# Down projection of a hybrid decoder block: the second half takes twelve of its 22 pairs of K tiles by seven products, in natural order, seven of them with stored differences

## The chip, the cores and the metric

One core of a Trainium2 chip runs the whole kernel. The time is device microseconds of one execution, from the kernel's start to its end; lower is better. Of the kernel before there are three timed runs: a median of 1657.48 us, between 1657.41 and 1657.68.

## The reference

The reference computes one decoder block on 256 tokens with a model width of 2048, in fp32. A projection of the input feeds two attention branches, which are projected, merged under gates and added to the input, with a layer norm behind them. Then comes the gated MLP with a hidden width of 5632, in which this case lies, a second layer norm, and a small per-layer embedding (PLE):

```python
x = layer_norm(ALPHA * x + out, ...)
# gated MLP: gate path with a causal depthwise conv of width 3, then GELU
h = gelu(conv(x @ W_gate)) * (x @ W_up)          # 256 x 5632
x = layer_norm(ALPHA * x + h @ W_down, ...)      # W_down: 5632 x 2048
x = x + sigmoid(x @ W_g) * (p @ W_p)
```

(The lines are shortened to what is computed.) The down projection is `h @ W_down`.

## The kernel before

**Numbers.** TensorE multiplies in a format with a shorter mantissa than fp32. So every fp32 operand is split in two parts: ScalarE (ACT) copies it into the short format, `hi` (line 117), and VectorE (DVE) subtracts that from the original, `lo` (line 226 for a classic unit, line 200 for a seven-product unit). A product of two operands is three matmuls: hi by hi, lo by hi, hi by lo.

**Stages.** The kernel goes through the value and key projections, gates, attention, two output projections, layer norm 1, gate and up projection (44 tiles of the hidden width), down projection, layer norm 2 and PLE. Weights come from DRAM as units of 1 MiB, each a pair of blocks of 512 KB, on SP's DMA queue. That queue is in order as the program writes it: a transfer whose buffer is still in use holds all that come after it. TensorE's order is the program's, too; the orders of VectorE, ScalarE and GpSimd (POOL) come from a scheduler.

**Down projection (lines 1373 to 1391 and `s_half`, 775 to 869).** The 5632 rows of W_down are 44 K tiles, taken as 22 pairs. The 2048 output columns are two halves of 1024 (`nh` = 0, 1), one after the other; each half goes over all 22 pairs, so a unit is a pair in a half. `DN_ORDER` gives the order of the pairs in each half. A pair is computed in one of two ways:

- *classic* (line 801): 2 K tiles x 2 token tiles x 2 column tiles x 3 matmuls = 24 matmuls of 128 x 512;
- *seven products* (`strassen`, line 809), for the pairs in `DN_S`: the 2 x 2 x 2 blocks by seven products in place of eight, 7 x 3 = 21 matmuls. The left operands need sums of the hidden activations, which the gate/up stage stores in DRAM (`sd`, line 1345) and which are loaded per unit (`hS`, line 193, 512 KB). The right operands need four differences of weight blocks on VectorE (line 154). Then a unit splits a block of 512 columns (b11), one of 1024 (b2) and two of 1024 with differences (t13, t24): four ACT copies and four lo subtractions, where a classic unit has two and two.

For the pairs in `DN_T` the differences are *stored* ("parked"): during the gate/up stage `park_gen` (lines 162 to 171) loads the 1 MiB unit, makes the four differences and stores the result by POOL's queue to `td` in DRAM. In the down projection such a unit loads 256 KB of raw weight (line 181), 512 KB (line 182), the stored 1 MiB `td` (line 184) and `hS`; one without loads two blocks of 512 KB (line 188) and `hS`. The pieces of `park_gen` are pulled at steps spread over the gate/up tiles from the seventh on (lines 1349 to 1351).

After the last seven-product pair of a half, `fold` (lines 815 to 834) adds the product sums that several output blocks share: one copy and eight VectorE operations on PSUM banks (lines 818 and 819).

**Buffers and lookahead.** `unit()` (line 234) prepares units three ahead of the one in use. Raw blocks of 512 KB go to a ring of five, hi and lo parts to rings of six each. hS, td, the hidden activations hC, the residual z, the layer norm's gains and the PLE operands share a pool of 15 tiles of 8 KB per partition. In the second half the last two pairs form a tail (`end2`, line 1395) that takes them by token tile and column tile, so that the layer norm can begin early.

**Other loads in the second half (line 1457).** After position 4 the half's residual `z` (2 x 512 KB, line 1366); after 8 the gains `lnb` (2 x 1 MiB, line 1159); after 14 `ple_prep` (praw 2 x 512 KB, line 1169; pTr 256 KB, line 1174; their splits are lines 1172 and 1177). In the first half the residual of that half is loaded after position 8, and nothing else.

Positions are counted from 0 in the order of the half. In the first half of the kernel before they are the natural order, with twelve seven-product pairs, six of them parked; in the second an order written out by hand, with nine, four of them parked.

Of the kernel before, what the change touches and what calls it, by code (L numbers as in the profile page):

```python
# [23 lines left out]
NF = DFF // P  # L24
# [28 lines left out]
WO_S = ((1, 3, 5), (1, 3, 5))  # L53
WO_C = (0, 2, 4, 6, 7)

DN_ORDER = (tuple(range(NF // 2)),
            (0, 1, 2, 3, 5, 4, 8, 9, 6, 11, 7, 12, 10, 14, 13, 15, 16, 17, 18, 19, 20, 21))
DN_S = ((1, 3, 5, 6, 8, 9, 11, 12, 14, 15, 17, 18), (1, 3, 5, 8, 9, 11, 12, 14, 15))


WO_T = ((3, 5), (1, 3, 5))
DN_T = ((3, 6, 9, 12, 15, 18), (5, 9, 12, 15))
PG_ORDER = (tuple(range(8)), tuple(range(8)))
PG_S = ((), (2, 4))
AFF1 = ((0, 2, 3), (0, 2))
# [9 lines left out]
def tile_block(ctx: ExitStack, tc: tile.TileContext, wu, wfv, wpp, xT_in, x_in, pT_in, wlr,  # L75
# [25 lines left out]
    def s8(shape, dt=F32, name=None):  # L101
        return big.tile(shape, dt, tag="S8", name=name)
# [23 lines left out]
    for _ in range(8):  # L126
# [7 lines left out]
               for b, order, sset in ((52, WO_ORDER, GV_S), (68, WO_ORDER, GR_S),  # L134
                                      (120, OUT_ORDER, WO_S), (dn0, DN_ORDER, DN_S),
                                      (NU - 16, PG_ORDER, PG_S))
# [3 lines left out]
    parked = {b + nh * len(order[nh]) + order[nh].index(n): None  # L140
              for b, order, tset in ((120, OUT_ORDER, WO_T), (dn0, DN_ORDER, DN_T))
              for nh in range(2) for n in tset[nh]}
    parked = {u: i for i, u in enumerate(sorted(parked))}
    td = dr.tile([len(parked), P, 2048], F32, name="td")
    sd = dr.tile([len(DN_S[0]), P, 1024], F32, name="sd")
    hS = {}
# [26 lines left out]
    def prep_s(u):  # L173
# [15 lines left out]
        if dn0 <= u < dn0 + NF:  # L189
            nh = (u - dn0) // (NF // 2)  # L190
            pair = DN_ORDER[nh][(u - dn0) % (NF // 2)]
            hS[nh, pair] = s8([P, 4, 256], F32R, name=f"hS{nh}_{pair}")
            nc.sync.dma_start(hS[nh, pair].bitcast(F32), sd[DN_S[0].index(pair)].rearrange(
                "p (i n) -> p i n", i=4))
# [148 lines left out]
    def pull(n, gens=mixers):  # L343
        for _ in range(n):
            while gens:
                try:
                    next(gens[0])
                    break
                except StopIteration:
                    gens.pop(0)  # L350
# [397 lines left out]
    def s_sums(y):  # L748

        a11, a21, a12, a22 = [y[:, k, t * P:t * P + P] for k in range(2) for t in range(2)]  # L750
        v = t2("sums").rearrange("p (i t) -> p i t", t=P)
        for i, a, b, op in ((0, a21, a22, ALU.add), (2, a21, a11, ALU.subtract),
                            (1, v[:, 0], a11, ALU.subtract), (3, a12, v[:, 1], ALU.subtract)):
            nc.vector.tensor_tensor(v[:, i], a, b, op)
        return v
# [548 lines left out]
    for n in range(NF):  # L1304
# [21 lines left out]
        if n % 4 == 0:  # L1326
            hC[n // 4] = (s8 if n < 40 else late.tile)([P, 4, 512], F32R, name=f"hC{n // 4}")
        if pair in DN_S[0]:
            if j == 0:
# [7 lines left out]
        nc.vector.tensor_tensor(dst[:, 256:512], h, dst[:, 0:256].bitcast(F32), ALU.subtract)  # L1337
        if pair in DN_S[0] and j == 1:
            v = s_sums(yp)
            for i in range(2):  # L1340
# [3 lines left out]
                                        w[:, :, 0:P].bitcast(F32), ALU.subtract)  # L1344
                nc.gpsimd.dma_start(sd[DN_S[0].index(pair), :, 512 * i:512 * i + 512],
                                    w.rearrange("p i n -> p (i n)").bitcast(F32))
        if n >= 4:
            pull(1)
        steps = 2 * sum(map(len, DN_T))
        if n >= n0 and (n - n0) * steps // (NF - 3 - n0) != (n - n0 + 1) * steps // (NF - 3 - n0):  # L1350
# [22 lines left out]
    def down(nh, tail, mid):  # L1373
# [9 lines left out]
        def ev(t, c, ps):  # L1383
            g = 2 * nh + c
            with tc.high_priority(P_STAT if tail else 0):
# [3 lines left out]

        s_half("dn", nh, DN_ORDER[nh], DN_S[nh], cl, st, z2of, ev,  # L1390
               tail, mid, end2, 1 if tail else 3)
# [155 lines left out]
def _sst(w, orders, ssets):  # L1547


    out = []  # L1550
    for nh, (order, sset) in enumerate(zip(orders, ssets)):
        for n in order:
            b = [[w[(2 * n + j) * P:(2 * n + j + 1) * P,
                    nh * 1024 + c * 512:nh * 1024 + c * 512 + 512] for c in range(2)]
                 for j in range(2)]
            out.append(np.concatenate([b[0][1], b[0][0], b[1][1], b[1][0]] if n in sset
                                      else b[0] + b[1], 1))
    return np.stack(out)
# [11 lines left out]
def _layout(i):  # L1570
# [4 lines left out]
    for n in range(16):  # L1575
        br.append(bg[n:n + 1])
        if n % 2 == 0:
# [7 lines left out]
        + [_sst(i["w_out"][0], OUT_ORDER, WO_S), gu,  # L1585
           _sst(i["w_down"][0], DN_ORDER, DN_S),
           _sst(i["w_ple_gate"][0], PG_ORDER, PG_S)], 0)
# [43 lines left out]
```

## Time and profile before

| | |
|---|---|
| median of three timed runs | 1657.48 us (1657.41 to 1657.68) |
| the profiled execution | 1657.66 us, of which the trace's span is 1655.9 |
| mean clock granted to TensorE | 0.999 |
| TensorE busy | 1648.5 us in 8875 matmuls |
| VectorE busy | 1326.3 us |
| ScalarE busy | 904.7 us |
| DMA | 391.6 MB, mean 236 GB/s over the span |
| down projection, first half | from 1329.63 us, 111.6 us |
| down projection, second half | from 1441.20 us to PLE's first matmul at 1554.76 |

How to read it: the profile is of one execution, on whose own time any sum has to be made. A row of the timeline gives start, duration, engine, line, operation, and output <- inputs. The duration of a matmul is longer than the distance between two of them, since they are pipelined; that distance is what counts. A row of a windows view gives the window, its length, the busy time of each engine with its instructions, then the granted clock, the busy share of the 16 DMA engines and the GB/s that they moved. In the DMA view a row ends with the size of each transfer and the median time from issue to landing.

### The profile page before, as it was taken

Reading aid. Unit: us, or ns where it says so; the run is one execution under the profiler, and the core shown is the slowest. Engines: PE = TensorE matmul, PEld = TensorE weight load, DVE = VectorE, ACT = ScalarE, POOL = GpSimd, SP = SyncE. Lnnn points to the kernel's source line nnn. Section 1 sums busy time; section 2 is a strip of 40 time slices with the busy share of each in tenths; the row PEclk is TensorE's granted clock in tenths of the full one; section 3 lists DMA queues with packets and bytes.
Section 4 is the critical chain, followed back from the end, with each engine's and each line's share of the span. In section 5 each row is a group of like instructions: output and inputs, shape, how many; then the busy total and the mean of one; then the engine's idle time right before and its main releaser. Section 6 shows DMA issues by size and latency. Waiting matters only on the chain.

```text
span 1655.9 us, 24358 instructions
## 1 busy us (share of the span) xinstructions
PE 1648.5 (100%) x8875; PEld 1432.1 (86%) x8875; DVE 1326.3 (80%) x2021; ACT 904.7 (55%) x1321; POOL 73.0 (4%) x214
## 2 busy tenths in 40 slices
PE   9999999999999999999999999999999999999998
PEld 8988888888888888888898888888888888888887
DVE  7666877888989868878987877777778778987787
ACT  6655555555555654545575455555545456555553
POOL 0100000000000000000010101100111000000000
PEclk9999999999999999999999999999999999999999
DMA  8755555545656557878856787778677679898564
GB/s 323 254 163 169 171 174 171 189 157 195 205 202 207 188 170 278 302 256 296 312 175 203 271 276 265 264 241 293 239 262 259 235 267 341 288 360 314 177 222 126
DMA packets 103175, 391.60 MB, mean 236 GB/s; under 512 B 11736, under 2 KB 13024, under 8 KB 96144
## 3 DMA queue, kind: packets, MB, share of 16 engines
q1 hardware_dynamic: 97872, 362.78, 64.3%
q0 software_dynamic: 5184, 27.27, 4.4%
q8 instruction: 69, 1.13, 0.3%
q14 instruction: 50, 0.41, 0.1%
HBM read 362.74 MB, written 27.27 MB: 236 GB/s over the span
## 4 chain that ended last, share of the span: by engine, by line
PE 98%; DVE 1%; DMA 0%; ACT 0%; issue 0%; POOL 0%; SPq 0%; DVEq 0%; POOLq 0%
PE dn L797 10%; PE psu L292 10%; PE psg L292 9%; PE psm L292 7%; PE psu L294 5%; PE psg L294 5%; PE gv L797 4%; PE gr L797 4%; PE wo L797 4%; PE psm L294 4%; PE psa L292 4%; PE dn_p L797 3%; PE pg L338 3%; PE fv L457 2%; PE psa L294 2%; PE psk L292 2%
## 5 line engine op out<-in xcount | busy, mean ns | idle before, releaser
L226 DVE TENSOR_TENSOR lo<-raw,hi 128x1024 fp32r<-128x1024 f32 x486 | 590.2, 1221 | 177.5 <-ACT hi L117 175.9
L117 ACT ACTIVATE hi<-raw 128x1024 fp32r<-128x1024 f32 x486 | 511.4, 1057 | 366.0 <-issue 151.9
L292 PE MATMUL psu<-x1T,hi 128*128 128x512 f32 x688 | 240.5, 392 | 0.0
L292 PE MATMUL psg<-x1T,hi 128*128 128x512 f32 x672 | 234.9, 392 | 0.0
L294 PE MATMUL psu<-x1T,lo 128*128 128x256 f32 x688 | 192.6, 280 | 0.0
L294 PE MATMUL psg<-x1T,lo 128*128 128x256 f32 x672 | 188.1, 280 | 0.0
L292 PE MATMUL psm<-xT,hi 128*128 128x512 f32 x512 | 181.5, 397 | 0.0
L292 PEld LDWEIGHTS psu<-x1T,hi 128*128 128x128 f32 x688 | 129.2, 188 | 27.4
L292 PEld LDWEIGHTS psg<-x1T,hi 128*128 128x128 f32 x672 | 126.2, 188 | 26.8
L294 PE MATMUL psm<-xT,lo 128*128 128x256 f32 x512 | 143.4, 280 | 0.0
L294 PEld LDWEIGHTS psu<-x1T,lo 128*128 128x128 f32 x688 | 130.6, 190 | 0.0
L294 PEld LDWEIGHTS psg<-x1T,lo 128*128 128x128 f32 x672 | 127.5, 190 | 0.0
L292 PEld LDWEIGHTS psm<-xT,hi 128*128 128x128 f32 x512 | 96.3, 188 | 19.6
L797 PE MATMUL dn<-hi,hC 128*128 128x512 f32 x368 | 102.3, 389 | 0.0
L117 ACT ACTIVATE hi_t<-raw 128x1024 fp32r<-128x1024 f32 x52 | 55.2, 1062 | 80.8 <-DVE raw L154 57.9
L117 ACT ACTIVATE hi_b<-raw 128x512 fp32r<-128x512 f32 x82 | 68.7, 841 | 54.9 <-DMA raw<-in_wu_dram 12.9
L294 PEld LDWEIGHTS psm<-xT,lo 128*128 128x128 f32 x512 | 97.2, 190 | 0.2
L200 DVE TENSOR_TENSOR lo_b<-raw,hi_b 128x512 fp32r<-128x512 f32 x82 | 77.8, 953 | 15.8 <-ACT hi_b L117 15.7
L292 PE MATMUL psa<-oT,hi 128*128 128x512 f32 x256 | 89.5, 392 | 0.0
L797 PEld LDWEIGHTS dn<-hi,hC 128*128 128x128 f32 x368 | 69.0, 188 | 14.3
L200 DVE TENSOR_TENSOR lo_t<-raw,hi_t 128x1024 fp32r<-128x1024 f32 x52 | 63.5, 1222 | 10.4 <-ACT hi_t L117 8.8
L294 PE MATMUL psa<-oT,lo 128*128 128x256 f32 x256 | 71.7, 280 | 0.0
(405 smaller groups left out, 3221.7 us busy)
## 6 DMA issues: line engine op xcount, KB each, us to landing
raw<-in_wu_dram SPq DMA_DIRECT2D x553, 512.0 KB, 5.1
td<-in_wu_dram SPq DMA_DIRECT2D x15, 1024.0 KB, 8.6
td<-td POOLq DMA_DIRECT2D x15, 1024.0 KB, 6.9
td<-td SPq DMA_DIRECT2D x15, 1024.0 KB, 8.2
hS<-sd SPq DMA_DIRECT2D x21, 512.0 KB, 8.4
fvraw<-in_wfv_dram SPq DMA_DIRECT2D x13, 524.0 KB, 6.6
sd<-hs POOLq DMA_DIRECT2D x24, 256.0 KB, 6.2
lnb<-in_lng_dram SPq DMA_DIRECT2D x4, 1024.0 KB, 9.8
```

The source lines that it names most:

```text
L117: return nc.scalar.activation(o, i, AF.Copy, bias=0.0, scale=scale)
L200: nc.vector.tensor_tensor(lo, src, hi.bitcast(F32), ALU.subtract)
L226: i = nc.vector.tensor_tensor(lo, raw, hi.bitcast(F32), ALU.subtract)
L292: nc.tensor.matmul(ps, lhsT=hi[i // 8 if hoff == 0 else 0][:, w0 % 1024:w0 % 1024 + P], rhs=a[:, kt % 4, :], start=first and i == 0, stop= ...
L294: nc.tensor.matmul(ps[:, 256:512], lhsT=lo[i // 8 if hoff == 0 else 0][:, w0 % 1024:w0 % 1024 + P], rhs=a[:, kt % 4, 0:256], start=False, ...
L338: nc.tensor.matmul(bs[j][:, 0:m], lhsT=x, rhs=v[:, o:o + m], start=first and i == 0, stop=last and i == 2)
L457: nc.tensor.matmul(fbk[t][c][:, 0:n], lhsT=x, rhs=w[:, o:o + n], start=kt == 0 and i == 0, stop=kt == 15 and i == 2)
L797: nc.tensor.matmul(ps[:, e], lhsT=x, rhs=w, start=todo[id(ps)] == total[id(ps)], stop=todo[id(ps)] == 1)
```

## The change

Only three tables at the head of the file change; the code that reads them is the same.

```diff
-DN_ORDER = (tuple(range(NF // 2)),
-            (0, 1, 2, 3, 5, 4, 8, 9, 6, 11, 7, 12, 10, 14, 13, 15, 16, 17, 18, 19, 20, 21))
-DN_S = ((1, 3, 5, 6, 8, 9, 11, 12, 14, 15, 17, 18), (1, 3, 5, 8, 9, 11, 12, 14, 15))
+DN_ORDER = (tuple(range(NF // 2)), tuple(range(NF // 2)))
+DN_S = ((1, 3, 5, 6, 8, 9, 11, 12, 14, 15, 17, 18),) * 2
...
-DN_T = ((3, 6, 9, 12, 15, 18), (5, 9, 12, 15))
+DN_T = ((3, 6, 9, 12, 15, 18), (3, 6, 9, 12, 14, 15, 18))
```

The first half stays as it is. In the second half pairs 6, 17 and 18 become seven-product pairs, the order becomes the natural one, pairs 3, 6, 14 and 18 become parked and pair 5 is no longer parked (it stays a seven-product pair with its differences made on the spot). So the half has 10 classic, 5 unstored and 7 parked pairs, where it had 13, 5 and 4. There are nine matmuls fewer, and three units more that `park_gen` loads, subtracts and stores in the gate/up stage. The fold of the second half comes behind position 18, where it came behind position 15. The weights in DRAM are laid out in the order of the units, ahead of the run.

## Prediction

> **What bounds the kernel now.** I read the page's totals and its chain first, then the waits of TensorE, then the timeline of the down projection, then its windows.
>
> ```profile
> span 1655.9 us, 24358 instructions
> ...
> PE 1648.5 (100%) x8875; PEld 1432.1 (86%) x8875; DVE 1326.3 (80%) x2021; ACT 904.7 (55%) x1321; POOL 73.0 (4%) x214
> ...
> PE 98%; DVE 1%; DMA 0%; ACT 0%; issue 0%; POOL 0%; SPq 0%; DVEq 0%; POOLq 0%
> ```
> ```profile
> PE warm_ps L127 <- DVE warm L124: 1.2, 1, 1.2
> PE fv L457 <- ACT fvhi L117: 0.3, 1, 0.3
> ```
>
> TensorE is busy for the whole span, and the second fence is the complete list of its waits: both are at the kernel's start, none is in the down projection. So the time is the count of matmuls times their pitch, as long as every operand is there in time. The change takes matmuls out and asks the DMA queue and VectorE for more in the same stretch; whether operands still come in time is the whole question. Pitch and pair times come from the timeline of the second half:
>
> ```profile
> 1446.64 0.39 PE L797 MATMUL dn_p<-hi_b,hC 128*128 128x512 f32 x1
> ...
> 1451.40 0.39 PE L797 MATMUL dn<-hi,hC 128*128 128x512 f32 x1
> ...
> 1456.84 0.39 PE L797 MATMUL dn_p<-hi_b,hC 128*128 128x512 f32 x1
> ```
>
> A seven-product pair (21 matmuls) lasts from 1446.64 to 1451.40, 4.76 us, and the classic pair behind it (24 matmuls) to 1456.84, 5.44 us: 0.227 us for a matmul, 0.68 us less for each pair that changes its kind. The second half begins one classic pair ahead of the first row, at 1441.20.
>
> **Term 1, the matmuls.** Three more pairs of the second half (6, 17 and 18; 3 x 3 = 9 matmuls) take seven products: 3 x 0.68 = 2.04 us less. All of it counts as long as TensorE never waits.
>
> **Term 2, the loads.** A classic pair loads 1 MiB. An unstored seven-product pair adds its 0.5 MiB of stored sums (hS): 1.5. A parked one loads 0.25 + 0.5 + 1 (td) + 0.5 = 2.25 MiB. The other loads of the stretch are the residual, the gains and the PLE operands. The sizes, in the DMA view of 1320 to 1560 us:
>
> ```profile
> raw<-in_wu_dram SPq DMA_DIRECT2D x77, 512.0 KB, 6.1
> td<-td SPq DMA_DIRECT2D x10, 1024.0 KB, 8.4
> hS<-sd SPq DMA_DIRECT2D x20, 512.0 KB, 8.4
> ...
> z<-x1d SPq DMA_DIRECT2D x4, 512.0 KB, 7.8
> lnb<-in_lng_dram SPq DMA_DIRECT2D x2, 1024.0 KB, 9.0
> praw<-in_wpp_dram SPq DMA_DIRECT2D x2, 512.0 KB, 8.1
> pTr<-in_pT_dram SPq DMA_DIRECT2D x1, 256.0 KB, 8.6
> ```
>
> Now the first half of before already runs this very order and choice of pairs (only pair 14 is unstored there), so it shows how such a half goes. Its single issues and landings, on SP's timeline and in the DMA view of each issue, with those of the second half's hS for its positions 6 and 15 behind them:
>
> ```profile
> 1346.06 0.37 SPq L193 DMA_DIRECT2D hS<-sd  x1
> hS<-sd SPq DMA_DIRECT2D x1, 512.0 KB, 9.0
> ...
> 1403.25 0.33 SPq L188 DMA_DIRECT2D raw<-in_wu_dram  x1
> raw<-in_wu_dram SPq DMA_DIRECT2D x1, 512.0 KB, 6.1
> ...
> 1457.47 0.42 SPq L193 DMA_DIRECT2D hS<-sd  x1
> hS<-sd SPq DMA_DIRECT2D x1, 512.0 KB, 6.8
> ...
> 1505.95 0.42 SPq L193 DMA_DIRECT2D hS<-sd  x1
> hS<-sd SPq DMA_DIRECT2D x1, 512.0 KB, 8.4
> ```
> ```profile
> 1415.36 0.39 PE L797 MATMUL dn_p<-hi_b,hC 128*128 128x512 f32 x1
> ...
> 1418.99 0.39 PE L797 MATMUL dn_p<-lo_t,hS 128*128 128x512 f32 x1
> ```
> ```profile
> 1415.92 1.23 DVE L200 TENSOR_TENSOR lo_t<-raw,hi_t 128x1024 fp32r<-128x1024 f32 x1 [1.21 <-ACT hi_t L117]
> ```
>
> In the first half the last load of position 6 lands at 1355.04, and pair 17's second weight block at 1409.3. From there to its last lo part (1415.92 + 1.23 = 1417.15) the split takes 7.8 us; TensorE wants that part at 1418.99, 3.63 us into the pair. So 1.84 us were left. The first half starts 85.7 us ahead of pair 17 (10 pairs of 4.76 and 7 of 5.44), at 1329.6: position 6 landed 25.4 us into the half.
>
> The second half after the change has the same positions 0 to 6, so I take 25.4 us there too. Pair 17's last part is wanted at 85.7 + 3.6 = 89.3 us, its block must land by 89.3 - 7.8 = 81.5 us: 56.1 us remain. In them the queue carries positions 7 to 16 and the two blocks of 17: 1 + 1.5 + 2.25 + 1 + 1.5 + 2.25 + 1 + 2.25 + 2.25 + 1 + 1 = 17 MiB, and with z (1), the gains (2) and the PLE operands (1.25) 21.25 MiB = 22.28 MB. That needs 397 GB/s. What the queue has given, in windows:
>
> ```profile
> 1355.04:1409.32 54.28, 54.28 (x241) 44.94 (x240) 46.31 (x49) 33.77 (x36) 0.00 (x0) 1.00 0.95 334
> ...
> 1464.30:1514.35 50.05, 50.05 (x222) 41.46 (x221) 39.93 (x43) 28.40 (x31) 0.00 (x0) 1.00 0.93 353
> ...
> 1464.30:1500.05 35.75, 35.75 (x159) 29.61 (x158) 29.04 (x31) 20.62 (x22) 0.00 (x0) 1.00 1.00 394
> ...
> 1500.05:1506.00 5.95, 5.95 (x28) 4.93 (x27) 5.53 (x7) 2.25 (x3) 0.00 (x0) 1.00 0.45 157
> ```
> ```profile
> 1499.97 0.33 SPq L181 DMA_DIRECT2D raw<-in_wu_dram  x1
> 1505.10 0.33 SPq L182 DMA_DIRECT2D raw<-in_wu_dram  x1
> ```
>
> The last three columns are the granted clock (full), the DMA engines' share and GB/s. The first half's stretch made 334 at a share of 0.95, with 4 MiB less to carry. The second half's made 353 over 50 us, but that is two regimes: 394 over 35.75 us in which the DMA engines were full, and 157 over 6 us in which SP, whose queue is in order, held its next block back from 1499.97 to 1505.10 until a buffer of the ring of five came free. At 353 the 22.28 MB take 63.1 us, 7.0 us too long; at 394 they take 56.5 us, 0.4 too long. When loads are late the buffers come free earlier relative to them, so such lulls should shrink, but a pair's raws are still held through a split of 7.8 us. I take the middle, 373 GB/s: 59.7 us, **3.6 us late**, which TensorE waits for at pairs 14 to 18. Ends for the range: 0 and 7.0.
>
> The Trainium skill, "DMA: Bandwidth & Descriptors", section Specifications, gives a limit of about 358 GB/s from HBM for one core; by it the load would take 62.2 us, be 6.1 us late and the change cost 4.9 us in all (an estimate from that page). The 394 over 35.75 us above speak against it as a limit. The skill's "HBM Reference", section Specifications (TRN2), says that a core that streams alone reaches about 425 GB/s; by that no load would be late, which is the first rival below. The 394 lie nearer to this one, the 353 to the other.
>
> **Term 3, the end of the half.** The fold of the seven products comes behind the last such pair: position 15 before, 18 now. Then one classic pair stands ahead of the tail's two instead of four, and VectorE has the fold, pair 18's split and three classic splits in a row. Spacings, from the first half's fold, which has that place already:
>
> ```profile
> 1421.08 1.22 DVE L226 TENSOR_TENSOR lo<-raw,hi 128x1024 fp32r<-128x1024 f32 x1
> 1422.21 0.68 DVE L818 SCALAR_TENSOR_TENSOR z<-z,dn_p 128x512 f32<-128x512 f32 x1
> 1422.81 2.35 DVE L226 TENSOR_TENSOR lo<-raw,hi 128x1024 fp32r<-128x1024 f32 x2
> ...
> 1434.95 0.68 DVE L200 TENSOR_TENSOR lo_b<-raw,hi_b 128x512 fp32r<-128x512 f32 x1
> ```
>
> A lo part of 1024 columns takes 1.13 us of VectorE's time (1421.08 to 1422.21), a fold step or a part of 512 columns 0.60 (1422.21 to 1422.81). In the built program's order six of the eight fold steps stand ahead of pair 21's second lo part. From pair 17's last lo: pair 18 0.6 + 3 x 1.13 = 4.0, six classic parts 6.8, six fold steps 3.6, together 14.4 us. TensorE, which goes over each token and column half in turn in the tail, wants that part 1.13 + 4.76 + 5.44 + 2.27 = 13.6 us after it: **0.8 us late**, if pair 17 was just in time. The first half does not pay this, as its last classic pairs are read whole. Bounds: 0, if VectorE is ahead at pair 17, and 1.2 (both fold steps more).
>
> **What I cost at nothing.** Three more parked units: each 1 MiB in, 1 MiB out through POOL and four subtractions in the gate/up stage.
>
> ```profile
> 1200.00:1329.00 129.00, 129.00 (x747) 114.16 (x746) 100.35 (x161) 64.92 (x99) 12.51 (x43) 1.00 0.70 244
> ```
> ```profile
> L154 DVE TENSOR_TENSOR td<-td 128x512 f32<-128x512 f32 x12 | 8.2, 686 | 3.7 <-DMA td<-in_wu_dram 3.7
> ```
> ```profile
> 1172.66 1.22 DVE L226 TENSOR_TENSOR lo<-raw,hi 128x1024 fp32r<-128x1024 f32 x1
> ```
> ```profile
> 1174.56 0.28 PE L294 MATMUL psg<-x1T,lo 128*128 128x256 f32 x1
> ```
>
> VectorE is busy 100 of 129 us there and the DMA engines 0.70; the three units add 3 x 4 x 0.69 = 8.2 us over the whole stage. TensorE's cover is thin where the subtractions fall between a unit's splits: the lo part that ends at 1173.88 is read at 1174.56, 0.68 us of cover. The built program has this pattern four times instead of twice, with the same instructions. If the cover is gone, each costs at most one subtraction, 0.7 us: 0 to 2.8 us, and I take 0. The further td, hS and store issues are SP's and POOL's; SP's are in term 2, POOL's queue is not read by anything before the down projection.
>
> **Sum.** Against the profiled execution, 1657.66 us (span 1655.9 and 1.8 around it, 0.18 above the median 1657.48): -2.04 + 3.6 + 0.8 = +2.4 us, 1660.0, and 1659.8 for the median.
>
> **Rivals.**
>
> *The queue keeps up* (1655.4 to 1657.9, chance 0.26): the engines stay full at 394 or more, nothing or up to 1.5 us is late, and -2.04 stands, with 0 to 0.8 of term 3. For it: 35.75 us at 394. Against it: no stretch as long as 56 us has done it, and the buffers leave the queue lulls.
>
> *The lulls stay* (1662 to 1665; worked out 1663.3, chance 0.21), the one on the other side: the ring of five raw blocks holds SP back as in the row of 157 GB/s, the whole stretch makes 353, and TensorE waits 7.0 us for pairs 14 to 18: -2.04 + 7.0 + 0.8 = +5.8. It decides from a lateness of 4.5 us on (rate under 368 GB/s), where the sum leaves the band below. For it: both halves' means, 334 and 353; a pair more with stored differences, 14, stands next to 15, 4.5 MiB in a row. And the lead shrank already in before: position 6's landing at 1464.3 was 7.5 us ahead of its pair (1441.20 + 3 x 4.76 + 3 x 5.44 = 1471.8), position 15's at 1514.35 3.0 us ahead of 1517.4.
>
> *A tile of the big pool is missing* (over 1665, chance 0.08): td and hS of the neighbours 14 and 15 wait for a pair of hidden activations to be used up, and all loads behind wait with them, a classic pair's 5.44 us: about 1665.4. For it: td, sums, residual and gains share one pool; against: no such wait shows in the first half with the same pairs.
>
> That the change does not do what it says: the built program has just nine matmuls fewer and three td stores more; 0.01, and the time would stay.
>
> **How the numbers follow.** The forecast's own cases (1.5 to 5.5 us late, 1657.9 to 1662) get 0.44. A difference of 0.2% (3.3 us, 1654.2 to 1660.8) is about what a measurement of this kernel tells from no change. Faster by more would need 3.3 us of gain where 2.04 are there: 0.02 for something unseen, taken half from the first rival, half from the forecast. Same: the first rival's 0.25 and a good half of the forecast's cases, 0.28, with 0.01: 0.54. Slower: the rest of the forecast's cases 0.15, 0.21 and 0.08: 0.44. The range from 1655.6 to 1665.4 leaves out the third rival and the edges.
>
> **What would show it.** Nine matmuls fewer at L797 and 2.04 us less busy time are sure. Right: rows of TensorE waiting in pairs 14 to 18, for lo_t or hi_b of L200 and L117 behind landings, some 3.6 us in sum, and one of about 0.8 for lo of pair 21; DMA windows of the half near 373 GB/s. Wrong: no wait at all (the queue gave 397), waits of hS or td issues behind TensorE (pool), waits in gate/up behind L154, or a first wait ahead of pair 9, which the volume does not explain.

## The result, and the profile after

The changed kernel takes 1660.11 us in the median of 21 runs (1658.77 to 1661.6), the kernel before 1657.66 (1656.78 to 1658.56) in the runs beside them: a ratio of 1.0015, 95% interval 1.0009 to 1.0021. That is 2.45 us more, within the 0.2% that was called no change. The forecast was 1659.8, or 2.4 us more. The profiled execution took 1659.76 us with a span of 1658.0, so it stands 0.35 us below its median.

The lines of the page are numbered one lower from the changed tables on (L796 is before's L797). Totals and chain of the changed kernel's page:

```profile
span 1658.0 us, 24401 instructions
...
PE 1648.0 (99%) x8866; PEld 1428.7 (86%) x8866; DVE 1337.0 (81%) x2039; ACT 908.1 (55%) x1327; POOL 78.5 (5%) x217
...
PE 97%; DVE 1%; ACT 0%; issue 0%; POOL 0%; DVEq 0%; ACTq 0%
```

There are nine matmuls fewer, and TensorE no longer fills the span. What it waits for, the whole list:

```profile
PE dn_p L796 <- ACT hi_t L116: 1.9, 2, 1.2
PE warm_ps L126 <- DVE warm L123: 1.2, 1, 1.2
PE dn L796 <- DVE lo L225: 0.8, 1, 0.8
PE dn_p L796 <- DVE lo_t L199: 0.2, 1, 0.2
```

All but the warm-up are new. On TensorE's timeline they stand where pair 17 and the tail are (start, duration, and in brackets the wait ahead and who ended it):

```profile
1328.95 0.40 PE L796 MATMUL dn<-hi,hC 128*128 128x512 f32 x1
...
1516.10 0.39 PE L796 MATMUL dn_p<-hi_b,hC 128*128 128x512 f32 x1
...
1521.28 0.39 PE L796 MATMUL dn<-hi,hC 128*128 128x512 f32 x1
...
1526.72 0.39 PE L796 MATMUL dn_p<-hi_b,hC 128*128 128x512 f32 x1
...
1528.71 0.50 PE L796 MATMUL dn_p<-hi_t,hS 128*128 128x512 f32 x1 [0.70 <-ACT hi_t L116]
...
1532.47 0.50 PE L796 MATMUL dn_p<-hi_t,hS 128*128 128x512 f32 x1 [1.15 <-ACT hi_t L116]
...
1533.73 0.50 PE L796 MATMUL dn_p<-lo_t,hS 128*128 128x512 f32 x1 [0.24 <-DVE lo_t L199]
...
1539.49 0.39 PE L796 MATMUL dn<-hi,hC 128*128 128x512 f32 x1
...
1544.71 0.62 PE L796 MATMUL dn<-hi,hC 128*128 128x512 f32 x2
...
1548.14 0.50 PE L796 MATMUL dn<-lo,hC 128*128 128x512 f32 x1 [0.76 <-DVE lo L225]
...
1556.89 0.39 PE L337 MATMUL pp<-pw,pTs 128*128 128x512 f32 x1
```

Read it by pairs. Pair 15 (1516.10 to 1521.28) lasts 5.18 us instead of 4.76. Pairs 17 and 18 (1526.72 to the classic pair at 1539.49) take 12.77 us instead of 9.52. With 0.1 us in pair 12 that is 3.8 us more than the matmuls need. The tail of two pairs begins with the second of the two matmuls that the row 1544.71 joins, at 1544.93, and ends at 1556.89: it takes 11.96 us for 48 matmuls that need 10.88: 1.1 us. The printed waits are shorter than these distances, since after each wait the next matmuls come a little slower. From the down projection's first matmul to PLE's first it is 227.94 us (1328.95 to 1556.89), where before had 225.13 (1329.63 to 1554.76): 2.81 more, that is -2.04 + 3.8 + 1.1. The 0.7 us by which the span grew less lies ahead of the down projection, which this run reached earlier.

The copy behind the second `hi_t` wait stood on ScalarE until VectorE had made its difference:

```profile
1531.36 1.06 ACT L116 ACTIVATE hi_t<-raw 128x1024 fp32r<-128x1024 f32 x1 [2.70 <-DVE raw L153]
```

Where pair 17's blocks come from: SP's timeline (the first row is two issues, 6.47 us apart from first start to last end), the DMA view of each of them, and the window from position 6's last landing (1465.13) to the second landing, 1521.12 + 4.4:

```profile
1514.99 6.47 SPq L187 DMA_DIRECT2D raw<-in_wu_dram  x2
1521.55 0.38 SPq L192 DMA_DIRECT2D hS<-sd  x1
...
raw<-in_wu_dram SPq DMA_DIRECT2D x1, 512.0 KB, 9.3
...
raw<-in_wu_dram SPq DMA_DIRECT2D x1, 512.0 KB, 4.4
```
```profile
1465.13:1525.55 60.42, 60.42 (x266) 49.36 (x265) 47.45 (x50) 36.49 (x40) 0.00 (x0) 1.00 0.96 365
```

The block landed 85.0 us into the half (which began at 1440.51); the prediction had needed 81.5 and expected 85.1. The queue gave 365 GB/s over 60.4 us; the prediction took 373 and 59.7. SP issued that block only at 1521.1, 6 us after the one ahead of it, but this hold cost nothing by itself: the block ahead landed at 1514.99 + 9.3 = 1524.3, and this one 1.25 us behind it.

In every trace here transfers that wait in the queue land, for the most part, 1.25 us apart for 512 KB: 419 GB/s. What goes beyond that pace I call a lull. By it the 21.25 MiB of the stretch need 53.1 us, and 7.3 of the 60.4 us are lulls, counted from the landings of the trace. 4.4 us of them stand ahead of four blocks that landed within 6 us of their own issue, so the queue had run dry; most of the rest stands ahead of transfers issued 7 to 11 us before, and its cause is open. The issues were late because SP waited for a raw block to be read by VectorE; the two largest rows of SP's waits in 1465.5 to 1521.2 us:

```profile
SPq L181 <- DVE lo L225: 8.5, 3, 3.0
SPq L221 <- DVE raw L153: 8.1, 2, 6.8
```

### The profile page after: what moved, and what is told of

Its sections match the earlier page's. It is cut to its first block, busy times and chain, and to the rows that moved or that the text cites. A ratio compares the mean times of both kernels' runs of the same rounds, so it can differ in the third digit from the quotient of the medians.

```text
span 1658.0 us, 24401 instructions
## 1 busy us (share of the span) xinstructions
PE 1648.0 (99%) x8866; PEld 1428.7 (86%) x8866; DVE 1337.0 (81%) x2039; ACT 908.1 (55%) x1327; POOL 78.5 (5%) x217
## 4 chain that ended last, share of the span: by engine, by line
PE 97%; DVE 1%; ACT 0%; issue 0%; POOL 0%; DVEq 0%; ACTq 0%
PE psu L291 10%; PE psg L291 9%; PE dn L796 9%; PE psm L291 7%; PE psu L293 5%; PE psg L293 5%; PE gv L796 4%; PE gr L796 4%; PE wo L796 4%; PE dn_p L796 4%; PE psm L293 4%; PE psa L291 4%; PE fv L456 3%; PE pg L337 3%; PE psa L293 2%; PE psfk L291 2%
## 5 line engine op out<-in xcount | busy, mean ns | idle before, releaser
L225 DVE TENSOR_TENSOR lo<-raw,hi 128x1024 fp32r<-128x1024 f32 x480 | 582.8, 1221 | 161.7 <-ACT hi L116 160.1
L116 ACT ACTIVATE hi<-raw 128x1024 fp32r<-128x1024 f32 x480 | 504.3, 1057 | 349.9 <-issue 126.2
L116 ACT ACTIVATE hi_b<-raw 128x512 fp32r<-128x512 f32 x88 | 73.7, 840 | 55.7 <-DMA raw<-in_wu_dram 12.7
L199 DVE TENSOR_TENSOR lo_b<-raw,hi_b 128x512 fp32r<-128x512 f32 x88 | 83.3, 954 | 17.4 <-ACT hi_b L116 17.2
L796 PE MATMUL dn<-hi,hC 128*128 128x512 f32 x320 | 89.3, 389 | 0.0
L796 PEld LDWEIGHTS dn<-hi,hC 128*128 128x128 f32 x320 | 60.0, 188 | 12.4
```

Source lines behind the costliest of these rows:

```text
L116: return nc.scalar.activation(o, i, AF.Copy, bias=0.0, scale=scale)
L199: nc.vector.tensor_tensor(lo, src, hi.bitcast(F32), ALU.subtract)
L225: i = nc.vector.tensor_tensor(lo, raw, hi.bitcast(F32), ALU.subtract)
L796: nc.tensor.matmul(ps[:, e], lhsT=x, rhs=w, start=todo[id(ps)] == total[id(ps)], stop=todo[id(ps)] == 1)
```

## The experiments

All runs stand beside runs of the kernel before on the same chip, whose median was between 1657.6 and 1657.8. Sums of waits are counted from each run's profile as the distances of the down projection's matmuls above 0.227 us, where they exceed it by 0.05 or more, so the slow restart is in them. By that count the changed kernel has 3.6 us in pairs 11 to 18 and 1.0 in the tail, the kernel before none. A profile is one execution of several: the changed kernel's 21 runs spread over 2.8 us.

**The gains out of the way.** `load_gain(1)` moves out of the hook behind position 8:

```diff
-        gain[1] = load_gain(1)
+    def gains():
+        gain[1] = load_gain(1)
...
-    down(1, 2, {4: lambda: load_z2(1), 8: late_loads, 14: lambda: pq.append(ple_prep(1))})
+    down(1, 2, {4: lambda: load_z2(1), 8: late_loads, 14: lambda: pq.append(ple_prep(1)),
+                19: gains})
```

> The changed kernel with the two gain loads (2 MiB) moved from behind position 8 to behind position 19, so that they no longer stand ahead of pairs 11 to 17 in SP's queue; VectorE's work keeps its place. Theory of the loads (the queue carries too much ahead of pair 17): at 394 GB/s 2.1 MB are 5.3 us, more than the 3.6 us that TensorE waits in pairs 14 to 18, so those waits go (0 to 0.5 left), the wait of about 1 at pair 21 stays, and the time is 3 to 3.6 us below the changed kernel, about 1656.8 (1.0 below before). Rival, VectorE's chain (pair 17's unstored split, with the PLE splits right ahead of it, is late by itself): pair 17 still waits 2 or more and the time is within 1 us of the changed kernel. Against both, the gains may land late for the layer norm and show as a new wait behind 1550 us.

Measured: 1656.67 us, ratio to before 0.9994 (0.9985 to 1.0003), 3.6 us below the changed kernel, each against its own runs of before. No wait is left in pairs 11 to 18; pair 17's block lands 81.9 us into the half, 3.1 us earlier. The gains are 5.0 us of transfers at the queue's pace; the lulls grew from 7.3 to 9.3 us. The tail's wait is still there, in this kernel's list of waits:

```profile
PE warm_ps L126 <- DVE warm L123: 1.2, 1, 1.2
PE dn L796 <- DVE lo L225: 0.8, 1, 0.8
```

So what stands in the queue ahead of pair 17 is the cause of the first group of waits, without any change of VectorE's work.

**Less of VectorE's work ahead of pair 17, the loads as they are.** In the second half's `ple_prep` the hi part stands in for the lo part:

```diff
-        w = [s8([P, 2048], F32R, name=f"pw{half}{i}") for i in range(2)]
+        w = [s8([P, 2048], F32R, name=f"pw{half}{i}") for i in range(2 - half)]
+        w = w + w[:half]
...
-            nc.vector.tensor_tensor(w[1][:, o], raw, w[0][:, o].bitcast(F32), ALU.subtract)
+            if half == 0:
+                nc.vector.tensor_tensor(w[1][:, o], raw, w[0][:, o].bitcast(F32), ALU.subtract)
```

> The changed kernel without the two lo subtractions of the PLE operands (2.4 us of VectorE right ahead of pair 17); the hi part stands in for the lo part in the PLE projection, so that part of the computation is changed. All loads stay. Theory of the loads: pair 17's blocks land when they did, its wait stays within 0.7 us (2 to 3 us in pairs 14 to 18), the time is within 0.7 us of the changed kernel. Rival, VectorE's chain: 2.4 us of its work is gone, the wait in pair 17 goes, 2 to 2.4 us below the changed kernel.

Measured: 1660.78 us, 1.0017 (1.0007 to 1.0026). The waits stay: 4.1 us in pairs 11 to 18, of them 1.0 in pairs 11 and 12 and 3.0 in pair 17 as in the changed kernel, and 1.1 in the tail. VectorE's 2.4 us are not what is short there.

**Pair 18 classic.**

```diff
-DN_S = ((1, 3, 5, 6, 8, 9, 11, 12, 14, 15, 17, 18),) * 2
+DN_S = ((1, 3, 5, 6, 8, 9, 11, 12, 14, 15, 17, 18),
+        (1, 3, 5, 6, 8, 9, 11, 12, 14, 15, 17))
...
-DN_T = ((3, 6, 9, 12, 15, 18), (3, 6, 9, 12, 14, 15, 18))
+DN_T = ((3, 6, 9, 12, 15, 18), (3, 6, 9, 12, 14, 15))
```

> The changed kernel with pair 18 classic: eleven seven-product pairs, six parked, the fold behind position 17, two classic pairs ahead of the tail. 0.68 us more of matmuls. Theory of the fold (term 3): the wait at pair 21 (0.9) goes, as VectorE gets a classic pair more of time, and the waits in pairs 14 to 17 stay at about 3 or grow none: 0.2 to 0.5 us below the changed kernel in sum. Rival, the tail's wait comes from the loads and not from the fold: the wait at pair 21 stays and the time is 0.7 above the changed kernel.

Measured: 1662.18 us, 1.0025 (1.0015 to 1.0035). The tail's wait is gone, as the theory of the fold said. The time is a miss: 1.9 us above the changed kernel instead of 0.2 to 0.5 below. Its profile shows where: 1.4 us of waits in pairs 11 and 12, 3.0 us in pair 17, and behind pair 17's last wait, of 1.28 us, 1.9 us in a stretch in which TensorE's granted clock was down. Windows of that kernel, ahead of, in and behind it:

```profile
1533.00:1534.65 1.65, 0.37 (x2) 0.00 (x0) 0.47 (x2) 1.11 (x2) 0.00 (x0) 1.00 0.37 117
1534.65:1536.05 1.40, 1.18 (x3) 0.74 (x4) 1.40 (x2) 1.40 (x2) 0.00 (x0) 0.72 0.67 237
1536.05:1538.90 2.85, 2.85 (x8) 2.21 (x8) 2.85 (x3) 2.34 (x3) 0.00 (x0) 0.54 0.60 172
1538.90:1542.00 3.10, 3.10 (x15) 2.54 (x15) 3.06 (x4) 1.06 (x1) 0.00 (x0) 1.00 0.91 324
...
1535.30:1538.70 3.40, 3.18 (x8) 2.48 (x8) 3.40 (x4) 3.09 (x4) 0.00 (x0) 0.50 0.55 166
```

The clock was at half for 3.4 us (the last row): eight matmuls in 2.85 us, then fifteen in 3.10 at full clock. Pairs 11 and 12 waited more than in the changed kernel, whose down projection is the same up to there. They stand at the edge in the changed kernel, too: its trace has the last lo part of pair 11 ready 0.2 us ahead of its matmul, the one with the gains late 4.4 us. In this run position 6's last block landed 25.4 us into the half instead of 24.6. The runs without the PLE's lo parts (26.7) and with pair 14 not parked (25.4) also wait at pair 11, 0.8 and 1.1 us. That fits a later start of the stretch, but only roughly, and was not tested.

**The parking alone.** In the kernel before:

```diff
-DN_T = ((3, 6, 9, 12, 15, 18), (5, 9, 12, 15))
+DN_T = ((3, 6, 9, 12, 15, 18), (5, 9, 12, 15, 16, 17, 18))
```

> The kernel before, with pairs 16, 17 and 18 of the second half parked as well though they stay classic: their differences are made and stored in the gate/up stage and never used. The down projection is that of before. Theory (parking is hidden, costed at nothing): the time of before, within 0.3 us, and no wait of TensorE in gate/up. Rival (the 0.7 us of cover is gone where subtractions fall between splits): 0.7 to 2.8 us more, with waits of TensorE for lo of the gate/up units.

Measured: 1657.43 us, 0.9998 (0.9989 to 1.0007), and no wait of TensorE in gate/up. Three more parked units cost nothing that shows in the median. The profiled execution is the slowest of the eleven, 1659.09 us, and has a wait of 0.3 us in the first half of the down projection.

**Both the PLE operands and the gains behind position 19.**

```diff
+    def gains():
+        pq.append(ple_prep(1))
+        gain[1] = load_gain(1)
...
-    down(1, 2, {4: lambda: load_z2(1), 8: late_loads, 14: lambda: pq.append(ple_prep(1))})
+    down(1, 2, {4: lambda: load_z2(1), 8: late_loads, 19: gains})
```

> The changed kernel with both the PLE operands (1.25 MiB and their splits, which stood behind position 14) and the gains (2 MiB) behind position 19, the PLE operands first. Theory of the loads: pair 17's block lands some 8 us earlier than in the changed kernel, no wait in pairs 11 to 18; VectorE is then ahead at pair 17 and has the PLE splits no longer in its way, so the wait at pair 21 goes as well (0 to 0.3 left): the whole 2.04 us of matmuls show, about 1655.8 beside 1657.8 of the kernel before. Rival (the tail's wait is the fold's and the splits' own and stays whatever the loads do): 0.8 to 1 us left at pair 21, about 1656.7. A third: the PLE splits land in VectorE's work of the layer norm and delay what follows 1550 us by 1 us or more.

Measured: 1656.39 us, 0.9992 (0.9983 to 1.0001). Its list of waits has none in the down projection:

```profile
PE warm_ps L126 <- DVE warm L123: 1.2, 1, 1.2
PE ptl L1107 <- DVE z L1097: 0.3, 1, 0.3
```

From the first matmul of the down projection to PLE's first it is 223.08 us (1329.53 to 1552.61), 2.05 below before: the matmuls' whole gain. From there to TensorE's last matmul it is 95.8 us, where before and the changed kernel have 95.1: 0.7 us are given back in the layer norm, into whose work on VectorE the PLE splits now fall. So 1.2 us are left. The tail's wait goes when VectorE is ahead at pair 17 (by 3.1 us here) and the PLE splits are out of its way; this run does not part the two.

**The PLE operands alone behind position 19,** the gains left behind 8.

```diff
-    down(1, 2, {4: lambda: load_z2(1), 8: late_loads, 14: lambda: pq.append(ple_prep(1))})
+    down(1, 2, {4: lambda: load_z2(1), 8: late_loads, 19: lambda: pq.append(ple_prep(1))})
```

> The changed kernel with only the PLE operands moved from behind position 14 to behind position 19; the gains stay behind 8. At the 366 GB/s that the changed kernel's queue gave from 1465 to 1525 us, 1.31 MB are 3.6 us. Theory of the loads: pair 17 is in time within 0.5 us, waits of at most 1 us in pairs 11 to 17, pair 21's wait at most 0.5; the time is 3 to 4.5 us below the changed kernel, 1655.8 to 1657. Rival (the gains are what hurts, since they stop the queue ahead of pairs 11 and 12 and the queue never recovers): waits of 2 us or more in pairs 11 to 18 stay.

Measured: 1663.3 us, 1.0034 (1.0022 to 1.0046). In the down projection it went nearly as expected: pair 17's block lands at 80.8 us, 0.3 us of waits in pairs 11 to 18, 0.7 in the tail instead of at most 0.5. But a new wait came, which the expectation had not:

```profile
PE pp L337 <- DVE pTs L1176: 3.8, 1, 3.8
```

The scheduler put the second lo part of the PLE's left operand behind the layer norm's steps on VectorE, and PLE's first matmuls wait for it. Behind this wait the clock was at half for 3.4 us:

```profile
1561.60:1565.00 3.40, 3.40 (x12) 2.65 (x10) 2.80 (x3) 0.00 (x0) 0.00 (x0) 0.50 0.47 136
```

From PLE's first matmul on, the run is 5.6 us longer than the changed kernel: 3.8 of wait, and most of the rest the slow clock. In the tail the PLE splits stand behind pair 21's lo parts here, and VectorE is 1.2 us ahead at pair 17; the tail's wait is shorter but stays. So the splits alone are not its cause. As to the loads, this run speaks for the theory of the loads by its waits, not by its time.

**Pair 14 not parked.**

```diff
-DN_T = ((3, 6, 9, 12, 15, 18), (3, 6, 9, 12, 14, 15, 18))
+DN_T = ((3, 6, 9, 12, 15, 18), (3, 6, 9, 12, 15, 18))
```

> The changed kernel with pair 14 of the second half not parked: 0.75 MiB less ahead of pair 17 and 2.8 us more of VectorE's differences in the half; one parked unit less. Theory of the loads: 0.79 MB at 366 GB/s are 2.1 us, so pairs 14 to 18 wait 1 to 2 us instead of 3.6, and the time is 1.5 to 2 us below the changed kernel. Rival, VectorE's chain: its 2.8 us more make the wait grow, 1 to 3 us above the changed kernel.

Measured: 1661.4 us, 1.0021 (1.0012 to 1.003). The waits are 3.9 us in pairs 11 to 18 and 1.1 in the tail: neither shorter by 2, as volume has it, nor 1 to 3 us longer, as VectorE's chain has it; the two stand 1.4 us apart with intervals that overlap. The rival's 1 to 3 us can be read into this time, but in the profiles the down projection is only 0.4 us longer than the changed kernel's. Its queue, again from position 6's last landing to that of pair 17's second block, and SP's two issues of pair 17:

```profile
1467.13:1527.90 60.77, 60.30 (x264) 49.03 (x263) 49.79 (x54) 36.49 (x40) 0.00 (x0) 1.00 0.95 348
```
```profile
1518.82 3.74 SPq L187 DMA_DIRECT2D raw<-in_wu_dram  x2
```

It took as long for less: 348 GB/s, and the block landed 86.2 us into the half, not 2.1 earlier. Volume at a fixed mean rate falls as the theory of the lateness. At 1.25 us for 512 KB the transfers are 1.9 us shorter, and the lulls 2.2 longer (9.5 us). A likely reason, not tested by itself: two raw blocks of pair 14 are now held through a long split, where the parked pair frees its raws early.

**A sixth raw block.** From this came the last question: is it the ring of five that holds SP back? Room is made by narrower lo tiles and smaller gaps between the pools, and a control takes that room without using it.

```diff
-GAPS = (96, 64, 80)
+GAPS = (8, 8, 80)
...
-        return rlo.tile([P, 1152], F32R, tag="lo", name=f"lo{name}")[:, o:o + 1024]
+        return rlo.tile([P, 1040], F32R, tag="lo", name=f"lo{name}")[:, o:o + 1024]
...
-    ring = ctx.enter_context(tc.tile_pool(name="ring", bufs=5))
+    ring = ctx.enter_context(tc.tile_pool(name="ring", bufs=6))
```

(The control has the first two parts only; with six, every tile of the ring says `bufs=6`.)

> The control: narrower lo tiles and smaller gaps alone, a ring of five. All theories: the time of the changed kernel within 1 us (about 1660). If it is faster or slower by more, the places of the buffers matter and the run with six is to be compared with this one.

> The changed kernel with a ring of six raw blocks instead of five; the room comes from narrower lo tiles (1040 columns, of which 1024 are used, instead of 1152) and smaller gaps between pools. The volume of the loads stays. After the run without pair 14's stored differences, in which 0.75 MiB less did not bring pair 17 forward, two theories of the load remain. Loop of the ring (SP holds blocks back until a raw block is split and free): a sixth block lets SP issue half a unit earlier, pair 17's second block lands 2 to 5 us earlier, the waits in pairs 11 to 18 fall to 0 to 1, and the time is 3 us or more below the changed kernel, 1656 to 1657.5. Rival, pure volume at 366 GB/s: the queue is as full as before, the block lands within 1 us of the changed kernel's 85 us into the half, the time within 1 us of 1660.

Measured: the control 1682.21 us, 1.0146 (1.0130 to 1.0161), six blocks 1680.31 us, 1.0135 (1.0121 to 1.0149). The control missed by far: moving the buffers alone costs 22 us, and six blocks can only be compared with it. TensorE is as busy as before, with more time from one matmul to the next; a classic pair on the control's timeline:

```profile
1512.25 0.40 PE L796 MATMUL dn<-hi,hC 128*128 128x512 f32 x1
...
1517.86 0.39 PE L796 MATMUL dn_p<-hi_b,hC 128*128 128x512 f32 x1
```

5.61 us instead of 5.44, 3% more. Against that control six blocks do what the loop of the ring said: waits of 2.7 us in pairs 11 to 18 become none, 0.8 in the tail become 0.5, and the block lands 81.1 us into the half instead of 86.7, with the same bytes. Of these 5.6 us, 3.0 are there at position 6 already (21.1 instead of 24.1 us) and 2.6 come in the stretch behind it, whose lulls fall from 9.5 to 6.9 us. SP's two issues of pair 17, control first, then six blocks:

```profile
1536.57 6.51 SPq L187 DMA_DIRECT2D raw<-in_wu_dram  x2
```
```profile
1531.63 4.08 SPq L187 DMA_DIRECT2D raw<-in_wu_dram  x2
```

**Six blocks and the gains behind position 19.** The two edits together.

> The ring of six with the gains behind position 19 as well. Theory: no wait in pairs 11 to 18, VectorE ahead by 2 us or more at pair 17, so the wait at pair 21 is gone or under 0.3: about 2 us below before, 1655.7. Rival (that wait is the fold's and no lead helps): 0.8 to 1 us stay there, about 1656.7.

Measured: 1679.97 us, 1.0132 (1.0119 to 1.0146): no wait in pairs 11 to 18 and 0.1 in the tail, on the slow pitch of the control. The lead at pair 17 was only 0.5 us, not 2, and since slower matmuls give VectorE more time, this does not show that a lead alone removes the tail's wait.

**The PLE operands early, the gains late.**

```diff
-    down(1, 2, {4: lambda: load_z2(1), 8: late_loads, 14: lambda: pq.append(ple_prep(1))})
+    down(1, 2, {4: lambda: load_z2(1), 8: lambda: (late_loads(), pq.append(ple_prep(1))),
+                19: gains})
```

> The changed kernel with the gains behind position 19 and the PLE operands behind position 8 instead of 14: the same loads ahead of pair 17 as with the gains late alone, but VectorE's PLE splits (3.2 us) stand ahead of pair 11, where 3 to 4 us of lead were left, and not ahead of pair 17. Theory (pair 21's wait is VectorE's, which has the PLE splits, pair 17's and 18's splits and the fold in one row): pair 17 gets 1 us or more of lead, the wait at pair 21 goes, nothing stays for the end, and the time is 2 us below before, about 1655.7. Rival: the splits take the lead of pairs 11 and 12, 0.5 to 2 us of waits there; the time is that of the gains late alone (1.0 below before) or above.

Measured: 1657.67 us, 0.9997 (0.9989 to 1.0006). The lead of pair 11 is eaten up, as the rival said (its last lo part is ready 0.1 us ahead of use). The profile has no wait above 0.1 us there and 0.7 in the tail, but it is the fastest of the eleven runs, 1656.35 us, 1.3 below their median; what the others wait for it does not show. By the median the rival's forecast came: not better than the gains late alone, 1.0 us worse.

**The order alone.** In the kernel before, with its nine seven-product pairs:

```diff
-            (0, 1, 2, 3, 5, 4, 8, 9, 6, 11, 7, 12, 10, 14, 13, 15, 16, 17, 18, 19, 20, 21))
+            tuple(range(NF // 2)))
```

> The kernel before with the second half in natural order, its nine seven-product pairs and four parked ones unchanged: same matmuls, same loads, other order. Theory (the load counts, not the order of the pairs): no wait of TensorE above 0.3 us, the time of before within 0.5 us. Rival (the order written by hand is what keeps before free of waits): waits in pairs 11 to 17, 1 us or more above before.

Measured: 1657.7 us, 1.0000 (0.9991 to 1.0009), no wait in the second half. The natural order costs nothing; what costs is what the three seven-product pairs more and their stored differences bring into the half.

## Why the prediction was right

*Term 1, the matmuls.* -2.04 us: exact. With all waits gone (both loads late) the down projection is 2.05 us shorter.

*Term 2, the loads, 3.6 us.* Measured 3.8, in pairs 12 to 18 and mostly 17. The place and the cause (what stands in SP's queue ahead of pair 17) are shown by the run with the gains late, which removes all of it, and by the one without the PLE's lo parts, which removes none. The waits were for `hi_t` twice and `lo_t` once, where the prediction had named lo_t or hi_b; the second hi_t stood behind VectorE's difference, so the split behind the landing counts as the sum had it (8.1 us from landing to last lo part, taken as 7.8).

That the sum came so near is in part luck. The landing of pair 17's second block at 85.0 us against 85.1 is two errors that cancel: position 6 landed at 24.6 us instead of 25.4, and the stretch took 60.4 us instead of 59.7. The reading "TensorE wants that part 3.6 us into the pair" took the matmuls in the order of the source, as in the first half of before. The description of the kernel before says that TensorE's order is the program's, but in the down projection `kernel.py` fixes it for the tail alone; elsewhere the scheduler sets it. In pair 17 of the changed kernel the trace has the last lo_t matmul 19th instead of 17th, so that part is wanted 0.45 us later than the sum had it.

And the step "22.28 MB at 373 GB/s" is right in size and not in kind. A mean rate is what comes out, not what limits. 394 GB/s, which the prediction took for full engines, is not the queue's full pace either; the run of the order alone has a stretch with more:

```profile
1465.00:1480.00 15.00, 15.00 (x68) 12.39 (x67) 11.69 (x13) 7.15 (x8) 0.00 (x0) 1.00 1.03 415
```

What the traces show is a sum of two parts: 512 KB each 1.25 us, and lulls of 6.6 to 9.5 us a stretch in the kernels with a ring of five. Bytes count in the first part. The second has a loop in it: SP waits for one of the five raw blocks, the block waits in the DMA queue behind what was issued before, then for the split, and then it is free. That the ring takes part in the lulls is shown by the sixth block, on the same bytes; that fewer bytes can be eaten up by longer lulls, by the run with pair 14 not parked. The rival "the lulls stay" had this mechanism and too high a price, 7.0 us; the middle between the two regimes happened to fall near what comes of both parts.

The two rules on bandwidth that the prediction weighed do not decide it. The Trainium skill, "DMA: Bandwidth & Descriptors", section Specifications, with its limit of about 358 GB/s, comes near the 365 of the stretch, but the queue's pace between lulls, 419 GB/s, is above it, and the ring of six, on the same bytes, ran ahead of it over its whole stretch, position 6 to pair 17:

```profile
1481.22:1541.21 59.99, 59.99 (x259) 48.33 (x258) 49.37 (x50) 38.52 (x42) 0.00 (x0) 1.00 0.98 374
```

The other rule's figure is near that pace, but a queue with lulls does not keep it up.

*Term 3, the fold, 0.8 us.* Measured 1.1: a printed wait of 0.76 for pair 21's second lo part, the very instruction, and a slow restart. With pair 18 classic it is gone, and with VectorE 3.1 us ahead and the PLE splits away it is gone too. How much lead is needed is open: with the PLE splits in their place and 0.5 us of lead the gains-late run keeps all of it, and with 1.2 us of lead and the splits away 0.7 us stay.

*Costed at nothing.* The parking is free by its own run. td and hS hardly waited for a tile of the pool: SP's waits in 1465.5 to 1521.2 us have 0.4 us ahead of a td and 0.5 ahead of hS that ended with TensorE, and SP issued pair 15's td 0.4 us behind the raw block ahead of it.

```profile
1505.30 0.33 SPq L181 DMA_DIRECT2D raw<-in_wu_dram  x1
1505.68 0.43 SPq L183 DMA_DIRECT2D td<-td  x1
```

The rival "the queue keeps up" came out neither way: with the gains late nothing is late in pairs 11 to 18, but with fewer bytes, at 350 GB/s and not at 394 or more.

A version ahead of both: with the gains, or the gains and the PLE operands, behind position 19 the medians are 1.1 and 1.2 us below before. That is clear of the changed kernel (3.6 us) but not of before: both intervals just include 1.

## What to carry to other kernels

When an in-order queue fills a small ring of buffers, ask of each transfer how long it keeps a later one from its buffer, and not only how many bytes there are: a load that is needed late and stands early delays what is needed soon (the gains, 5.0 us of transfers, by 3.1 us here). When a change takes work off a saturated engine and adds loads, look for loads in that stretch that nothing needs yet. And a run that moves buffers needs a control that moves them without the rest.

## What the runs showed of the hardware

Where the tiles lie in memory changed the matmuls' pitch: with lo tiles of 1040 instead of 1152 columns and smaller gaps, and nothing else, a classic pair took 5.61 us instead of 5.44 and the kernel 22 us more. Which of the two did it was not tried.

One DMA queue of one core moved 512 KB each 1.25 us, 419 GB/s, for the most part of the time in which it had transfers waiting; its means over 50 to 60 us were 334 to 374 GB/s, with lulls in between.

Several short waits can bring the clock down: in the run with pair 18 classic, waits of 0.56, 0.27 and 1.28 us within 5 us were followed by 3.4 us at half clock, worth 1.9 us. The Trainium skill, "TensorE: Matmul & The Clock Gate", section "Why this matters for your kernels", warns of gaps above about 3 us; the 3.8 us wait of the run with the PLE operands alone late agrees (3.4 us at 0.50 behind it), and this trace shows the same for several shorter ones. The changed kernel's own profile has waits of 0.70, 1.15 and 0.24 us at the same place, the same sum, and kept a clock of 1.00, so it does not always come.
